# The first modulation's weights by tiles of 128 features, and three blocks of the first product row by row

## The chip, the cores and the metric

The kernel runs on one core of one Trainium2 chip. What is measured is the time of one execution on the device in microseconds (us). The kernel before takes 1365.48 us, the median of three runs (1364.51 to 1366.25).

## The reference

Three transformer layers for one sequence of 256 tokens with 1024 features, in float32. The first layer is an attention with a branch of pooled tokens beside it, then a gated feed-forward with a short convolution; the second has forgetting and sliding-window attention, the third a selected attention and eight experts. Every layer is modulated: a vector c gives, by a product with a weight of 1024 rows and 6144 columns, a shift, a scale and a gate for each of the two halves of the layer. What the change touches is the beginning:

```
mod = silu(c) @ ada_w + ada_b            # 6 x 1024: shift1, scale1, gate1, ...
h   = rms_norm(x, norm1_g) * (1 + scale1) + shift1
z   = h @ w_in                           # q, k, v, pooled part, two gates
q   = rms_norm(heads(q), q_norm_g);  k = rms_norm(heads(k), k_norm_g)
logits = q k^T * scale + bias_table[distance]
```

No column of z can be finished before all 1024 features of h are there, and a feature of h needs its own column of shift1 and of scale1.

## The kernel before

**Layout.** Features lie on partitions: x is four tiles of 128 x 2 x 256, eight "rows" of 128 features by 256 tokens. Every product with a weight is made in three float32r passes: weights and features are both split into a high part (ScalarE, `split_hi`, line 195) and a low part (VectorE, `split_lo`, line 198), and `mm3` (lines 214 to 216) multiplies high by high, high by low and low by high. One block of w_in (256 columns, 1 MB) is 48 matmuls of 256 columns: eight rows of features, two halves, three passes.

**The weights.** `Stream` holds one list of loads, `plan`. Each load is up to 1 MB into one of five buffers called `raw`, issued from the SP queue (line 89). A load is issued in the code whenever a buffer is handed out (`take`), and waits for the reader of the buffer that it overwrites. Weights of kind "w" are split ahead of their use into `whi` and `wlo`; the modulation's weights ("ada", "fill") are used whole.

**The modulation.** 8 MB hold shift1 and scale1: group 0 of layer 0, in eight pieces of 128 rows of ada_w by 2048 columns. `ada_step` (sum at line 344) multiplies each by silu(c), copied to 32 columns (`cb`), four matmuls of 512 columns on four strips of the array. The sums are complete when the eighth piece is through; `ada_turn` then turns them to columns by four transposes (line 368) and adds the bias (line 370).

**The order at the start.** `run` calls `setup` (column vectors, five loads of modulation weights, x, the first 128 columns of the constants), `rope_tables` (tables of sine and cosine for a later layer), five sums, `t5_table` (the bias table by distance, written to memory and read back), the sums of squares of x (line 473), a sixth sum. `layer1` then calls `norm_first`: the reciprocal root, the split of w_in block 0, two more sums, the turn, and eight features, each by three operations (lines 465, 466, 468). After that come the reads of the bias table (line 741), the other constants (line 785, with the matrices "blk" and "flip"), the bands of the pooling (line 760), and the blocks 0 (q), 2 (k) and 4 (v) of w_in one after the other. Behind a block, work that was put off is done by `flush`: for q and k the mean square by heads, a product with "blk" (line 798), followed by three ScalarE and three VectorE operations (lines 400 to 408, 800). Then `t5_end` turns the bias round by four products with "flip" (line 750), and `weave` runs the heads, whose scores (line 564) start, between further blocks.

**What sets the order.** The program is written with a layer that makes the semaphores and orders each engine's instructions by when they become ready and by their place in the code. Two engines are exempt: in all of this part ScalarE keeps the order of the code (`ORDER`: main "a"), and inside the block "start" TensorE keeps it (start "p").

Of the kernel before, what the change touches and what calls it, by code (L numbers as in the profile page):

```python
# [9 lines left out]
F32 = mybir.dt.float32  # L10
# [6 lines left out]
T = 256  # L17
# [5 lines left out]
_COLS = {}  # L23
# [47 lines left out]
class Stream:  # L71
    """Weights in the order of their loads: loaded ahead, split into two float32r parts ahead.
    The modulations' weights ("ada") take part whole; those of a kind "fill" wait until they are asked for."""
# [10 lines left out]
    def load(self, upto=None):  # L84
        """As many as there is room for"""
# [54 lines left out]

    def next(self, key, ahead=None, finish=True):
# [11 lines left out]
class Kernel:  # L153
# [84 lines left out]
    def gemm_t_steps(self, key, h, kt, n=256, fine=False):  # L238
        """[n columns of w on partitions (two tiles a bank), tokens]"""
# [17 lines left out]
    def gemm_t2(self, keys, h):  # L257
        """Blocks of 256 columns, a row of h at a time as it is made"""
# [10 lines left out]
    def flush(self):  # L269
        """Work put off so that the tensor engine needn't wait for it"""  # L270
# [7 lines left out]
    def gemm_n_steps(self, key, h, fine=False):  # L278
        """[tokens on partitions (two tiles), 256 columns of w]"""
# [15 lines left out]
    def gemm_narrow(self, hi, lo, h):  # L295
        """[8 columns of w on partitions, tokens]"""
# [18 lines left out]
    def ada_step(self, layer, g, kt, raw, defer, weigh):  # L315
        """128 rows of a group of modulations' weights. weigh: on the vector engine, summed over the rows later"""
# [41 lines left out]
    def ada_turn(self, a):  # L358
        """The sums, on every 32nd partition, go to a column for each 128 of them"""
# [14 lines left out]
    def ada_finish(self, upto=None):  # L374
        """One step of what is left to do for the oldest group, or all that a group needs"""
# [19 lines left out]
    def rstd(self, ps, shape, first=None):  # L395
        """-2 / root of a mean square; the gains make up for the -2. first: a factor that goes ahead, in place"""
# [22 lines left out]
    def norm_begin(self, gain, layer=None, scale_i=None):  # L419
        """The norm that follows the coming updates of x"""  # L420
# [16 lines left out]
    def norm_sum_first(self, k):  # L437
        n = self.nrm
        if k % 2 == 0:
            n["sq"][k // 2] = self.big()  # L440
        self.nc.scalar.activation(n["sq"][k // 2][:, k % 2], self.x[k // 2][:, k % 2], AF.Square)
        self.norm_sum(k)

    def norm_first(self):
        """The first norm: the modulation is the last to come"""
        nc, n = self.nc, self.nrm
        r = self.rstd(n["ms"][:, 0], (slice(None), 0))
        xr = []
        for i in range(4):
            xr.append(self.big())  # L450
            nc.vector.tensor_tensor(xr[i], self.x[i], r[:, None, :].to_broadcast([128, 2, T]), op=OP.mult)
        self.S.split(1)
        self.S.ada(2)
        self.ada_finish()
        gs = self.sp.tile([128, 8], F32, name="gs", bufs=2)
        nc.vector.scalar_tensor_tensor(gs, self.mods(0, 1), 1.0, self.gain("n1"), op0=OP.add, op1=OP.mult)
        shift = self.mods(0, 0)
        hh, hl = [], []
        for i in range(4):
            th, tl = self.big(F32R), self.big(F32R)  # L460
            hh.append(th)
            hl.append(tl)
            for j in range(2):
                k = 2 * i + j
                nc.scalar.activation(th[:, j], xr[i][:, j], AF.Identity, scale=gs[:, k:k + 1], bias=shift[:, k:k + 1])  # L465
                nc.vector.tensor_scalar(xr[i][:, j], xr[i][:, j], gs[:, k:k + 1], shift[:, k:k + 1], op0=OP.mult,
                                        op1=OP.add)
                nc.vector.tensor_tensor(tl[:, j], xr[i][:, j], th[:, j].bitcast(F32), op=OP.subtract)  # L468
        return hh, hl
# [65 lines left out]
    def acc_end(self, key, act, gate, n_ada):  # L535
        """The last rows: each feature tile goes on into the stream and its norm"""
# [33 lines left out]
    def attend(self, q, k, v, add, pair, sink=None, after=None):  # L570
        """One head, a stage at a time; a pair's second one ends both"""
# [62 lines left out]
    def pair_out(self):  # L634
        """Where two heads' results meet, and their split for the product that follows"""
# [18 lines left out]
    def setup(self):  # L654
# [4 lines left out]
        self.S.load()  # L659
# [1040 lines left out]
```

## Time and profile before

| | |
|---|---|
| median of the runs | 1365.48 us (1364.51 to 1366.25) |
| profiled execution, first to last instruction | 1360.7 us |
| TensorE busy | 1311.9 us, 96% |
| TensorE, loading of weights into the array | 1166.2 us, 86% |
| VectorE busy | 970.2 us, 71% |
| ScalarE busy | 737.6 us, 54% |
| read and written | 342.81 MB, mean 252 GB/s |

All times in the rows are of the profiled execution, from its first instruction on; the runs' median contains some 4.8 us beside that span. PE is TensorE, DVE is VectorE, ACT is ScalarE. SPq is the queue of SyncE, which issues the loads. In a timeline a row can stand for several instructions (x4), the second number is the time from the start of the first to the end of the last, and in brackets stands how long the engine was idle before it and what ended that. Matmuls are pipelined, so the distance between two starts, not the length of one, tells what one costs in a sequence. A float32 matmul stands there twice.

### The profile page before, as it was taken

The page shows a single profiled execution, that of the slowest core. Times are in us where ns is not written, and L with a number is a line of the kernel's source. Part 1 is how long each engine was busy: PE and PEld are TensorE (multiplying, and loading weights), DVE is VectorE, ACT ScalarE, POOL GpSimd, SP SyncE. Part 2 cuts the span into 40 slices and gives each one's busy share as a digit, 9 for nine tenths or more (in the row PEclk, how much of TensorE's full clock was granted, in tenths as well). Part 3 has the DMA queues.
Part 4 walks back from the last instruction along what each step waited for, and adds up shares of the span by engine and source line. Part 5 has one row for each costly group of instructions (what it writes and reads, how often), then busy time and mean ns, then how long its engine had stood idle before and what let it go on. Part 6 is the DMA issues. An engine that isn't in the chain of part 4 may idle for free. (4 is left out here: it accounts for less than half of the span.)

```text
span 1360.7 us, 22311 instructions
## 1 busy us (share of the span) xinstructions
PE 1311.9 (96%) x9230; PEld 1166.2 (86%) x9230; DVE 970.2 (71%) x1411; ACT 737.6 (54%) x928; POOL 4.1 (0%) x11
## 2 busy tenths in 40 slices
PE   5999999999999999999999999989999999999995
PEld 1777998899998887799999888669899899999994
DVE  3646865666567566666656579678889889889885
ACT  3645464544445454544334442656776776776773
POOL 0000000000000000000000000000000000000000
PEclk8899999999999999999999999999999999999997
DMA  9856947676664722577757553124998998997990
GB/s 370 333 194 245 407 188 274 232 284 233 266 226 188 302 97 76 192 300 301 279 216 278 193 225 109 48 93 177 351 355 293 350 374 283 341 371 276 348 374 34
DMA packets 54141, 342.81 MB, mean 252 GB/s; under 512 B 6061, under 2 KB 7349, under 8 KB 22928
## 3 DMA queue, kind: packets, MB, share of 16 engines
q1 hardware_dynamic: 53792, 341.02, 66.3%
q8 instruction: 74, 1.21, 0.4%
q0 software_dynamic: 240, 0.29, 0.2%
q14 instruction: 35, 0.29, 0.1%
HBM read 340.23 MB, written 1.06 MB: 251 GB/s over the span
## 5 line engine op out<-in xcount | busy, mean ns | idle before, releaser
L198 DVE TENSOR_TENSOR wlo<-raw,whi 128x2048 fp32r<-128x2048 f32 (+2 forms) x309 | 571.0, 1864 | 135.3 <-ACT whi L195 134.4
L195 ACT ACTIVATE whi<-raw 128x2048 fp32r<-128x2048 f32 (+2 forms) x309 | 482.7, 1573 | 181.8 <-PE ps L216 87.0
L214 PE MATMUL ps<-b,whi 128*128 128x256 f32 x1740 | 501.3, 289 | 1.2 <-ACT b L465 1.1
L215 PE MATMUL ps<-b,whi 128*128 128x256 f32 x1740 | 493.6, 284 | 0.5 <-DVE b L468 0.3
L216 PE MATMUL ps<-b,wlo 128*128 128x256 f32 x1740 | 493.1, 284 | 0.0
L214 PEld LDWEIGHTS ps<-b,whi 128*128 128x128 f32 x1740 | 333.7, 192 | 33.5 <-issue 16.1
L215 PEld LDWEIGHTS ps<-b,whi 128*128 128x128 f32 x1740 | 334.6, 192 | 3.2 <-issue 1.3
L216 PEld LDWEIGHTS ps<-b,wlo 128*128 128x128 f32 x1740 | 334.1, 192 | 1.8 <-issue 0.9
L215 PE MATMUL ps<-wlo,b 128*128 128x384 f32 (+2 forms) x800 | 267.0, 334 | 3.9 <-DVE wlo L198 3.9
L214 PE MATMUL ps<-whi,b 128*128 128x384 f32 (+2 forms) x800 | 267.0, 337 | 0.0
L216 PE MATMUL ps<-whi,b 128*128 128x384 f32 (+2 forms) x800 | 265.3, 332 | 0.0
L215 PEld LDWEIGHTS ps<-wlo,b 128*128 128x128 f32 x800 | 151.1, 189 | 13.7 <-DVE wlo L198 6.9
L214 PEld LDWEIGHTS ps<-whi,b 128*128 128x128 f32 x800 | 150.5, 189 | 9.0 <-issue 2.9
L216 PEld LDWEIGHTS ps<-whi,b 128*128 128x128 f32 x800 | 151.0, 189 | 7.3 <-issue 0.3
L344 PE MATMUL ps<-raw,cb 128*32 128x512 f32 x424 | 66.9, 639 | 14.3 <-DVE cb L672 9.4
L904 ACT ACTIVATE b<-ps,cols 128x256 f32<-128x256 f32 x44 | 24.7, 563 | 82.8 <-PE ps L216 53.5
L585 ACT ACTIVATE prob<-prob,tiny 128x128 f32<-128x128 f32 x80 | 35.7, 448 | 37.8 <-DVE tiny L580 20.7
L204 ACT ACTIVATE b<-b 128x512 fp32r<-128x512 f32 x24 | 15.2, 632 | 65.5 <-DVE b L929 44.6
L905 DVE SCALAR_TENSOR_TENSOR b<-ps,cols,b 128x255 f32<-128x255 f32 x44 | 21.2, 482 | 35.4 <-ACT b L904 35.3
L344 PEld LDWEIGHTS ps<-raw,cb 128*32 128x32 f32 x424 | 10.9, 111 | 38.9 <-DMA raw<-in_ada 13.5
L328 DVE SCALAR_TENSOR_TENSOR ada_acc<-raw,sc,ada_acc 128x2048 f32<-128x2048 f32 x16 | 37.5, 2347 | 4.6 <-DMA raw<-in_ada 4.5
L514 DVE SCALAR_TENSOR_TENSOR x<-ps,mod,x 128x256 f32<-128x256 f32 x72 | 31.1, 475 | 6.2 <-PE ps L216 5.8
(256 smaller groups left out, 977.8 us busy)
## 6 DMA issues: line engine op xcount, KB each, us to landing
raw<-in_ada SPq DMA_DIRECT2D x72, 1024.0 KB, 5.0
raw<-in_ed SPq DMA_DIRECT2D x40, 1024.0 KB, 7.7
raw<-in_eg SPq DMA_DIRECT2D x48, 768.0 KB, 5.6
raw<-in_eu SPq DMA_DIRECT2D x48, 768.0 KB, 5.5
raw<-in_w_up SPq DMA_DIRECT2D x22, 1024.0 KB, 5.5
raw<-in_w_in SPq DMA_DIRECT2D x16, 1024.0 KB, 7.0
raw<-in_w_down SPq DMA_DIRECT2D x11, 1024.0 KB, 6.8
raw<-in_e_fg SPq DMA_DIRECT2D x11, 1024.0 KB, 5.3
```

The costliest lines, as they stand in the source:

```text
L195: self.nc.scalar.activation(hi[:, c], raw[:, c], AF.Copy)
L198: self.nc.vector.tensor_tensor(lo[:, c], raw[:, c], hi[:, c].bitcast(F32), op=OP.subtract)
L204: nc.scalar.activation(hi, src, AF.Copy)
L214: mm(ps, ah, bh, start=start, stop=False, skip_group_check=True)
L215: mm(ps, ah, bl, start=False, stop=False, skip_group_check=True)
L216: mm(ps, al, bh, start=False, stop=stop, skip_group_check=True)
L328: nc.vector.scalar_tensor_tensor(a["acc"], raw, self.sc[:, c:c + 1], a["acc"], op0=OP.mult, op1=OP.add)
L344: self.nc.tensor.matmul(ps[32 * j:32 * j + 32, :], weights, rows[:, j * 512:(j + 1) * 512], start=start, stop=stop, skip_group_check=True)
L514: self.nc.vector.scalar_tensor_tensor(x, ps, gate[:, k:k + 1], x, op0=OP.mult, op1=OP.add)
L585: nc.scalar.activation(p[:, c], p[:, c], AF.Exp, bias=mn[:, t:t + 1], scale=-1.0, accum_out=sm[:, t:t + 1])
L904: nc.scalar.activation(y[:, j], ps[:, j], AF.Identity, scale=cw(2, j), bias=self.col("cb", base + j))
L905: nc.vector.scalar_tensor_tensor(y[:, j, 1:], ps[:, j, :T - 1], cw(1, j), y[:, j, 1:], op0=OP.mult, op1=OP.add)
```

## The change

The weights of shift1 and scale1 are laid out anew: `ada0f` holds eight tiles, tile k with all 1024 rows of the 128 shift columns and the 128 scale columns that feature row k needs. So one megabyte finishes one row of h. For each tile, `first_sums` makes eight matmuls of 256 columns, two on each of four strips of the array; `first_row` copies the four partial sums, adds and turns them by two matmuls with a column `pick` of zeros and four ones, adds the bias, makes the gain and finishes the features of the row with the three operations of before. `first_products` writes out the order: the sums of tile k, then the matmuls of blocks 0, 2 and 4 of w_in for row k - 1 (block 2 joins at tile 3, block 4 at tile 4 with the rows that it has missed), then the turn of tile k. The T5 table is made behind tile 4's turn. The plan loads tile 0, block 0, tile 1, block 2, tile 2, block 4, then tiles 3 to 7, then the rest as before. x is loaded ahead of the weights, and squared in tiles of 512. The constants are loaded in one piece where the second piece was loaded. The norm of q and of k, and the copy of v, follow the three blocks together; then one block of weights is split and the put-off work flushed. The rotary tables move to the second round of the first feed-forward. `first_row` uses the norm's result `xr` in place, as before.

```diff
@@ class Stream
+    def first(self):
+        raw = self.take(self.adas[self.n_a])
+        self.n_a += 1
+        return raw
@@ class Kernel
+    def first_sums(self, k):
+        nc = self.nc
+        raw, ps = self.S.first(), self.psum()
+        for kt in range(8):
+            j = 32 * (kt % 4)
+            nc.tensor.matmul(ps[j:j + 32, 0], self.cb[:, kt], raw[:, kt * 256:kt * 256 + 256], start=kt < 4,
+                             stop=kt >= 4, skip_group_check=True)
+        self.S.load()
+        return ps
+
+    def first_row(self, k, ps):
+        nc = self.nc
+        row = self.big()[:, 0]
+        nc.scalar.activation(row, ps[:, 0], AF.Copy)
+        for c in range(2):
+            nc.tensor.matmul(ps[:, 1, c:c + 1], row[:, c * 128:c * 128 + 128], self.pick, start=True, stop=True)
+        mod, gs = self.mod[0], self.gs0
+        o = _COLS["ab0"][0]
+        nc.vector.tensor_tensor(mod[:, k:16:8], ps[:, 1, 0:2], self.cols[:, o + k:o + 16:8], op=OP.add)
+        nc.vector.scalar_tensor_tensor(gs[:, k:k + 1], mod[:, 8 + k:9 + k], 1.0, self.gain("n1")[:, k:k + 1],
+                                       op0=OP.add, op1=OP.mult)
...
+        x, th, tl = (t[k // 2][:, k % 2] for t in (self.xr, *self.h0))
+        nc.scalar.activation(th, x, AF.Identity, scale=gs[:, k:k + 1], bias=mod[:, k:k + 1])
+        nc.vector.tensor_scalar(x, x, gs[:, k:k + 1], mod[:, k:k + 1], op0=OP.mult, op1=OP.add)
+        nc.vector.tensor_tensor(tl, x, th.bitcast(F32), op=OP.subtract)
+
+    def first_products(self):
+        S, h = self.S, self.h0
+        blocks = []
+
+        def weights(i, tokens):
+            blocks.append((self.parts(S.next(("w_in", i), 1, False), 8, 256), self.psum(), tokens))
+
+        def rows(b, ks):
+            (hi, lo), ps, tokens = blocks[b]
+            for k in ks:
+                for m in range(2):
+                    c = slice(m * 128, m * 128 + 128)
+                    if tokens:
+                        self.mm3(ps[:, m], h[0][k // 2][:, k % 2, c], h[1][k // 2][:, k % 2, c], hi[:, k], lo[:, k],
+                                 k == 0 and m == 0, k == 7)
+                    else:
+                        self.mm3(ps[:, m], hi[:, k, c], lo[:, k, c], *self.row(h, k), k == 0 and m == 0, k == 7)
+
+        self.first_row(0, self.first_sums(0))
+        weights(0, False)
+        for k, after in ((1, ((0, (0,)),)), (2, ((0, (1,)),)), (3, ((1, (0, 1)), (0, (2,)), (1, (2,)))),
+                         (4, ((2, (0, 1, 2)), (0, (3,)), (1, (3,)), (2, (3,)))),
+                         *((k, tuple((b, (k - 1,)) for b in range(3))) for k in (5, 6, 7)),
+                         (8, tuple((b, (7,)) for b in range(3)))):
+            if k < 8:
+                ps = self.first_sums(k)
+            for b, ks in after:
+                rows(b, ks)
+            if k < 8:
+                self.first_row(k, ps)
+            if k in (1, 2):
+                weights(2 * k, k == 2)
+            if k == 4:
+                self.t5_table()
+        self.flush()
+        return [ps for _, ps, _ in blocks]
@@ setup
-        self.S.load()
         self.x = [self.ap.tile([128, 2, T], F32, name=f"x{i}") for i in range(4)]
         for i in range(4):
             nc.sync.dma_start(self.x[i], d["xT"][:, 2 * i:2 * i + 2, :])
+        self.S.load()
         self.cst = self.cp.tile([128, N_CONST], F32, name="cst")
-        nc.sync.dma_start(self.cst[:, :128], d["cst"][:, :128])
@@ layer1
-    def layer1(self):
-        nc, x, S = self.nc, self.x, self.S
-        h = self.norm_first()
+    def layer1(self, first):
+        nc, S, h = self.nc, self.S, self.h0
         self.t5_begin()
-        nc.sync.dma_start(self.cst[:, 128:], self.d["cst"][:, 128:])
+        nc.sync.dma_start(self.cst, self.d["cst"])
         self.pool_bands()
...
-        qk_norm(0, *self.gemm_t2((("w_in", 0),), h))
-        self.whole(qk_piece(2))
-        self.whole(v_piece(0))
+        qk_norm(0, first[0])
+        qk_norm(2, first[1])
+        vn[0] = self.copy_out(first[2])
+        self.S.split(1)
+        self.flush()
         self.t5_end()
@@ ffn
+            if i == 1 and conv:
+                self.rope_tables()
@@ plan
-        plan += [("fill",) + x[1:] for x in ada[0][:6]] + l1[:1] + [("fill",) + x[1:] for x in ada[0][6:8]]
-        put(l1[1:], ada[0][8:24], 3)
+        first = [("first", k, d["ada0f"][k], 2048) for k in range(8)]
+        for k in range(3):
+            plan += [first[k], l1[k]]
+        plan += first[3:]
+        put(l1[3:], ada[0][8:24], 1)
@@ run
-                self.rope_tables()
...
-                S.ada(5)
-                self.t5_table()
-                for k in range(8):
-                    self.norm_sum_first(k)
-                S.ada(1)
+                for i in range(4):
+                    self.norm_squares(i)
+                    self.norm_sums(i)
+                self.norm_first()
+                first = self.first_products()
```

## Rows read from the trace of the kernel before

**Rows 1.** The page, part 1: TensorE's busy time, share, instructions; its weight loads; other engines.

```profile
PE 1311.9 (96%) x9230; PEld 1166.2 (86%) x9230; DVE 970.2 (71%) x1411; ACT 737.6 (54%) x928; POOL 4.1 (0%) x11
```

**Rows 2.** Timeline of TensorE, 15 to 64 us: start us, us, operation, idle before.

```profile
15.95 1.07 PE L344 MATMUL ps<-raw,cb 128*32 128x512 f32 x8 [0.85 <-DMA raw<-in_ada]
18.46 1.93 PE L344 MATMUL ps<-raw,cb 128*32 128x512 f32 x8 [1.45 <-DMA raw<-in_ada]
20.33 1.45 PE L729 MATMUL ps<-prob,rb 33*8 33x384 f32 x2
...
31.26 1.53 PE L344 MATMUL ps<-raw,cb 128*32 128x512 f32 x8 [1.42 <-DMA raw<-in_ada]
33.49 1.12 PE L368 MATMUL ps<-cst,b 128*128 128x128 f32 x4 [0.70 <-ACT b L356]
35.70 0.58 PE L214 MATMUL ps<-b,whi 128*128 128x256 f32 x1 [1.10 <-ACT b L465]
36.61 0.58 PE L215 MATMUL ps<-b,whi 128*128 128x256 f32 x1 [0.33 <-DVE b L468]
...
37.20 0.41 PE L214 MATMUL ps<-b,whi 128*128 128x256 f32 x1
37.42 0.41 PE L215 MATMUL ps<-b,whi 128*128 128x256 f32 x1
...
45.06 0.28 PE L214 MATMUL ps<-b,whi 128*128 128x256 f32 x1
45.18 0.28 PE L215 MATMUL ps<-b,whi 128*128 128x256 f32 x1
...
50.79 1.10 PE L798 MATMUL ps<-b,cst 128*128 128x512 f32 x2 [0.17 <-DMA cst<-in_cst]
...
57.47 1.02 PE L798 MATMUL ps<-b,cst 128*128 128x512 f32 x2
58.33 3.60 PE L750 MATMUL ps<-b,cst 128*128 128x512 f32 x8
...
63.34 0.46 PE L564 MATMUL ps<-b 64*128 64x128 f32 x2 [1.41 <-DVE b L800]
```

**Rows 3.** Busy time by stretch: TensorE, its loads, DVE, ACT, POOL, granted clock, DMA.

```profile
30.00:32.00 2.00, 0.74 (x8) 0.16 (x8) 2.00 (x5) 0.20 (x1) 0.00 (x0) 0.93 1.02 426
...
40.00:42.00 2.00, 2.00 (x11) 2.00 (x11) 1.97 (x5) 2.00 (x2) 0.96 (x2) 0.51 1.01 418
42.00:44.00 2.00, 2.00 (x19) 2.00 (x19) 2.00 (x2) 0.70 (x1) 0.12 (x1) 1.00 0.93 331
...
1346.00:1348.00 2.00, 0.00 (x0) 0.00 (x0) 0.69 (x1) 0.07 (x1) 0.00 (x0) 0.50 0.03 8
```

**Rows 4.** SP's queue: timeline of its loads, then its longest waits up to 70 us.

```profile
20.46 13.94 SPq L89 DMA_DIRECT2D raw<-in_w_in  x3
...
35.40 2.26 SPq L741 DMA_DIRECT2D b<-t5tab  x4
37.71 0.59 SPq L785 DMA_DIRECT2D cst<-in_cst  x1
39.02 8.22 SPq L760 DMA_DIRECT2D b<-in_band  x4
...
SPq L89 <- DVE wlo L198: 5.6, 1, 5.6
SPq L89 <- PE ps L344: 4.9, 2, 4.2
```

**Rows 5.** Timelines of DVE and ACT: a feature's low part, and two of a norm's steps.

```profile
35.69 0.41 DVE L466 TENSOR_SCALAR b<-b,gs,mod 128x256 f32<-128x256 f32 x1 [0.67 <-ACT b L465]
...
58.53 0.69 ACT L400 ACTIVATE b<-ps,eps 128x512 f32<-128x512 f32 x1 [2.21 <-PE ps L798]
...
59.91 0.63 ACT L402 ACTIVATE b<-b 128x512 f32<-128x512 f32 x1
```

**Rows 6.** The page, part 6: the modulation's loads, KB each, median us to landing.

```profile
raw<-in_ada SPq DMA_DIRECT2D x72, 1024.0 KB, 5.0
```

More of the change, by code (lines that the diff above doesn't have):

```diff
@@ L435, in norm_feed, with norm_squares @@
             nc.vector.tensor_scalar(n["xg"][i][:, j], self.x[i][:, j], n["gs"][:, k:k + 1], None, op0=OP.mult)
-    def norm_sum_first(self, k):
+    def norm_squares(self, i):
         n = self.nrm
[L439 to L442, printed above, removed]
+        n["sq"][i] = self.big()
+        self.nc.scalar.activation(n["sq"][i], self.x[i], AF.Square)
     def norm_first(self):
@@ L447, in norm_first @@
         r = self.rstd(n["ms"][:, 0], (slice(None), 0))
-        xr = []
+        self.xr = []
         for i in range(4):
[L450 to L468, printed above, removed]
@@ L469, in norm_first @@
-        return hh, hl
+            self.xr.append(self.big())
+            nc.vector.tensor_tensor(self.xr[i], self.x[i], r[:, None, :].to_broadcast([128, 2, T]), op=OP.mult)
+        self.mod[0] = self.cp.tile([128, 48], F32, name="mod0")
+        self.gs0 = self.sp.tile([128, 8], F32, name="gs", bufs=2)
+        self.h0 = ([], [])
+    def first_sums(self, k):
[7 more added lines that the diff above has]
+        return ps
@@ new lines, in first_row @@
+    def first_row(self, k, ps):
[9 more added lines that the diff above has]
+                                       op0=OP.add, op1=OP.mult)
+        if k % 2 == 0:
+            for part in self.h0:
+                part.append(self.big(F32R))
+        x, th, tl = (t[k // 2][:, k % 2] for t in (self.xr, *self.h0))
+        nc.scalar.activation(th, x, AF.Identity, scale=gs[:, k:k + 1], bias=mod[:, k:k + 1])
+        nc.vector.tensor_scalar(x, x, gs[:, k:k + 1], mod[:, k:k + 1], op0=OP.mult, op1=OP.add)
+        nc.vector.tensor_tensor(tl, x, th.bitcast(F32), op=OP.subtract)
@@ L674, in setup @@
         nc.vector.memset(self.ones, 1.0)
+        self.pick = self.cp.tile([128, 1], F32, name="pick")
+        nc.vector.memset(self.pick, 0.0)
+        for j in range(4):
+            nc.vector.memset(self.pick[32 * j:32 * j + 1], 1.0)
     def rope_tables(self):
@@ L1513, in run @@
                 self.norm_begin("n1")
-                S.ada(5)
-                self.t5_table()
-                for k in range(8):
-                    self.norm_sum_first(k)
-                S.ada(1)
+                for i in range(4):
[3 more added lines that the diff above has]
+                first = self.first_products()
             self.nsink = self.cp.tile([128, 8], F32, name="nsink")
             nc.vector.tensor_scalar(self.nsink, self.col("sink", 0, 8), -1.0, None, op0=OP.mult)
-            h = self.layer1()
+            h = self.layer1(first)
             self.ffn(h, ("w_up", "w_up2", "w_down"), self.mods(0, 5), True, lambda: self.norm_begin("en1", 1, 1))
@@ L1651, in _layout @@
         d[f"ada{l}"] = _ada(a[name][0])
+    w = a["ada_w"][0][:, :2048].reshape(8, 128, 2, 8, 128)
+    d["ada0f"] = np.ascontiguousarray(w.transpose(3, 1, 0, 2, 4)).reshape(8, 128, 2048)
     d["w_in"] = _by_cols(a["w_in"][0])
```

## The prediction

> **What bounds the kernel now.** I read the page's busy shares first: TensorE is busy for 1311.9 of 1360.7 us [rows 1], so all idle time together is 48.8 us, and no change that keeps the multiplications can win more. Then TensorE's timeline of the first 64 us, where the change lies. The reader is to see three stretches. Until 31.26 us TensorE waits for the modulation's megabytes, which land every 2.5 us (15.95, 18.46) [rows 2]; eight of them, x and one block of w_in are needed. From 35.70 it multiplies without a hole, one matmul each 0.21 us until about 41.9, then one each 0.12 us [rows 2]: the granted clock is at half (1.2 GHz) up to 42 us, after a stretch in which the engine was mostly waiting, and full (2.4 GHz) behind it [rows 3]. The three blocks end at 57.47, two products with the constant "blk" stand between and behind them, four with "flip" follow, and the first scores start at 63.34 [rows 2]. From there on TensorE has hardly a gap until the end. So **63.34 us is the number to beat**: what the change moves that point by, it moves the end by.
>
> Third, SP's timeline: loads leave in the order in which the program names them. For 13.9 us SP sits at three loads of w_in, mostly waiting for buffers that TensorE (4.9 us in all) and VectorE (5.6) have yet to read, and does not send the free loads of constants and bands meanwhile; those go out at 35.40, 37.71 and 39.02, in program order [rows 4]. The constants arrive just in time: "blk" waits 0.17 us for them at 50.79 [rows 2].
>
> **The change part by part.** Durations are those of the one profiled execution (span 1360.7 us); the runs' median lies 4.8 us above it, outside the work shown, and I add the difference to the median.
>
> *Arrival.* x takes the place that the first megabyte had. That one landed at 18.46 - 4 x 2.5 = 8.5 us; then come first0, w_in 0, first1, w_in 2, first2, w_in 4, first3 at 11.0, 13.5, ... 26.0. Two more megabytes (w_in 2 and 4) now lie before the last modulation tile, so DMA alone would bring that at about 36 us instead of 31.26 [rows 2].
>
> *TensorE from 26.0 on.* Before first3 little can be multiplied: 12 of the 144 matmuls. From there the written order makes TensorE the bound, and I sum it at full clock:
> - five sums of a tile, 5 x 1.07 = 5.4 (eight matmuls of 256 columns for four of 512: the same columns) [rows 2];
> - five turns of a row by two products with "pick". No row has them; above, the four transposes (1.12 at half clock, so 0.56) and below, nothing, as pick could lie in another's shadow [rows 2]. I take the transposes: 2.8;
> - the T5 table, now in here: 1.45 at half clock, 0.7 [rows 2];
> - 132 matmuls at 0.12: 15.8 [rows 2];
> - waits for the feature. From a finished turn it is mod, gain, high part on ScalarE, and the low part. Before, the turn ended at 34.6, the first matmul started at 35.70 and the second, which needs the low part, at 36.61 [rows 2]: 2.0 us. The low part's first step waits for ScalarE, 0.67 us [rows 5]. For tiles 4 to 6 a sum of 1.07 covers about half, 0.9 each is left; behind tile 7 nothing covers it. 3 x 0.9 + 1.9 = 4.6. If VectorE and ScalarE run ahead it is 0, at most 2.0 each, 10.
>
> Sum 29.3, so 55.3 us. Half clock: up to 26 us the engine works in shorter pieces than before, so I count one recovery as at 35.7 to 41.9, 6.2 us x (1 - 0.12/0.21) = 2.7 [rows 2, 3]; bounds 0 and the whole stretch. The three blocks end at **58.0 us**, not earlier than before: the hole is filled, but the sums' two halves, the chain of eight features and the extra turns eat it.
>
> *The constants.* This is what becomes late. "blk" and "flip" are now loaded whole behind the first product's code, so behind fifteen loads, the last of which (w_in 5) reuses the buffer of first7. Its sum ends two rounds of 18 matmuls, one turn and one feature's chain before the end: 58.0 - 2 x 2.2 - 0.5 - 1.9 = 51.2. From there a megabyte takes 5.0 us [rows 6] and lands at 56.2. Behind it come the T5 bias and the constants. Before, w_in 3 landed at 31.26 + 5 x 2.5 = 43.8 and the constants at 50.8, 7.0 us for both [rows 2, 4]; at the full 2.5 us a megabyte it would be 4.4. I take 7.0, the measured one: **63.2 us**. TensorE stands 5 us for "blk" (0 if the loads go out earlier, 7 at most).
>
> *What follows in place of the block that stood between.* Before, "blk" for q ran 6.7 us ahead of that for k, with a block between. Now both stand together: the first takes 1.1, then two chains of three ScalarE steps (58.53 to 60.54, 2.0 each), then VectorE's three for k up to the score at 63.34, 2.8 behind [rows 2, 5]: 1.1 + 4.0 + 2.8 = 7.9. The scores start at **71.1 us**, 7.8 later than before. TensorE's own 5.8 us (two "blk", four "flip") end 2.1 before that; matmuls of w_in 1, split by then, can fill it, since TensorE's order outside the start is found by readiness. That gives back between 0 and 2.1; I take 2.0. Net +5.8.
>
> *The stall's own price.* Near the end, where TensorE stands still from 1346 to 1348 us, its clock is at half [rows 3]. So behind a stall of 5 us "blk" and "flip" may run at half, up to 3 us more. I leave it out of the sum, since no row shows what a stall of just this length does, and keep it in the range.
>
> *Beside other work.* The rotary tables leave the start for the second round of the first feed-forward: nine VectorE and three ScalarE operations of 0.3 to 0.5 us, under a TensorE that has none of it in its own queue; cover gone, the price is their sum, some 4 us. x first, Squares of 512 for 256, the merged constants load, the memsets of pick: off the path, as x is there 2.5 us before the first tile. ScalarE has one block's split less done ahead at the scores; w_in 3's 4.2 us of splitting then lies under 48 matmuls. Zero, at most 2. The end of the program is untouched.
>
> **Where a rule speaks against it.** The clock rows show recovery after six unbroken microseconds [rows 3]; whether rounds of sums, waits and 18 matmuls count as unbroken no row shows. If TensorE stayed at half through them, 132 matmuls and five sums would take 16.7 us more than at full clock (132 x 0.09 + 5 x 0.9): the blocks end at 55.3 + 16.7 = 72, the last sum 10.4 before that at 61.6, the constants land at 73.6 and the scores start at 81.5, net +16 with the fill. The Trainium skill's "TensorE: Matmul & The Clock Gate", section "HAM oscillation — how this bites in real kernels", says that a loop whose computing per tile is shorter than its wait for the next tile falls back in clock on every tile. By that rule the trace agrees for the stretch before 31 us; after first3 the wait is the shorter one, so I give it little.
>
> **Rivals.** *Constants in time, net nothing*: SP sends them while it waits for buffers, or TensorE takes w_in 1 during the stall. Then the scores start 7.9 behind 58.0 at 65.9, less the fill of 2.0: +0.5 us, 1366. For it: nothing binds "blk" to the weights. Against it: SP's order before [rows 4]; and w_in 1 is split by ScalarE only behind the three blocks.
>
> *Faster*: the chain of features is hidden and the clock stays full from 26.0 on, with constants at 56 or before. 26.0 + 5.4 + 2.8 + 0.7 + 15.8 = 50.7, scores at 58.6, less 2.0: -6.7; with half of the feature waits and half of the recovery left, -3 to -4; I write 1361. It decides at whether SP's constants go out before the sum of tile 5, about 42 us. For it: ScalarE and VectorE are two thirds idle there. Against: in-place writing makes the low part wait for the high part [rows 5].
>
> *Clock at half throughout*: +16 us, 1382, as above. That the change doesn't overlap at all is no rival: the matmuls of tile 3 on can't be kept from running between loads.
>
> **How the numbers follow.** Forecast, slower by 3 to 10 us, 0.52; half clock throughout, 0.06; within 0.2% (2.7 us, about what can be told from no change), 0.21; faster, 0.21. The likeliest: 1365.5 + 5.8 = **1371.3 us**, its own range 1368.2 to 1375.5. The range for all, 1360.5 to 1377, leaves out the half-clock case and the better half of the faster one's tail.
>
> **What would show it.** Right: w_in 5's load leaves SP only after the sum of tile 7, near 51 us; the wait of "blk" for the constants is the largest of TensorE behind 26 us, about 5; the third block ends near 58; the first score starts near 71, and from there the two traces run alike. Wrong: constants landing before the third block ends, a score before 63 us, or a granted clock that stays full between 20 and 34 us; and a wait in the first feed-forward would show the rotary tables uncovered.

## The result: 12 us slower

The changed kernel takes 1377.27 us, the median of four runs (1375.75 to 1378.43), beside 1364.99 for the kernel before (four runs): a ratio of 1.0096, 95% interval 1.0080 to 1.0113. The forecast was 1371.3 with a range up to 1377, so the sign was right, the size about half of what came, and the result lies just past the end of the range. The profiled execution took 1376.16 us over a span of 1374.4, so 1.8 lie beside the span. The span of before was 1360.7; if 1.8 lay beside that too, it was a quick execution of some 1362.5, and not 4.8 us lay outside it as the text above says. Differences of spans below are therefore some 1.4 us larger than those of medians: 13.7 for 12.3.

TensorE's page line shows that 8.2 of the 13.7 us are busy time (1320.1 for 1311.9 in [rows 1]), so idle time is the smaller part of the loss. It has 92 more records: 64 of the tiles' sums, which come in halves, and 28 of the turns, which take 4.9 us together for the 1.12 of [rows 2]. Matmuls at half clock, shown further down, are busy for longer too:

```profile
PE 1320.1 (96%) x9322; PEld 1174.2 (85%) x9322; DVE 973.1 (71%) x1428; ACT 740.0 (54%) x929; POOL 4.0 (0%) x11
```

TensorE's timeline of the start, after, columns as in [rows 2] (L531 are the norm's sums, L466 a tile's sums, L477 a turn, L220 to L222 the three passes, L858 "blk", L811 "flip", L622 scores, L350 a later modulation's sums, L659 transposes in the heads):

```profile
8.61 5.04 PE L531 MATMUL ps<-b,ones_d 128*128 128x256 f32 x12 [0.96 <-ACT b L446]
13.58 1.07 PE L466 MATMUL ps<-raw,cb 128*32 128x256 f32 x16
...
21.26 0.58 PE L220 MATMUL ps<-b,whi 128*128 128x256 f32 x1 [3.45 <-ACT whi L201]
23.59 0.58 PE L222 MATMUL ps<-b,wlo 128*128 128x256 f32 x1 [1.53 <-DVE wlo L204]
...
29.61 1.93 PE L466 MATMUL ps<-raw,cb 128*32 128x256 f32 x16
...
46.00 0.50 PE L477 MATMUL ps<-pick,b 128*128 128x1 f32 x4
...
48.56 0.39 PE L221 MATMUL ps<-b,whi 128*128 128x256 f32 x1 [0.52 <-DVE b L489]
...
50.70 0.50 PE L477 MATMUL ps<-pick,b 128*128 128x1 f32 x4
51.13 1.07 PE L466 MATMUL ps<-raw,cb 128*32 128x256 f32 x16
52.63 0.38 PE L220 MATMUL ps<-b,whi 128*128 128x256 f32 x1 [0.42 <-ACT b L487]
...
57.32 0.38 PE L220 MATMUL ps<-b,whi 128*128 128x256 f32 x1 [1.15 <-ACT b L487]
...
60.23 0.28 PE L222 MATMUL ps<-whi,b 128*128 128x256 f32 x1
63.23 2.74 PE L858 MATMUL ps<-b,cst 128*128 128x512 f32 x4 [2.72 <-DMA cst<-in_cst]
65.77 4.55 PE L811 MATMUL ps<-b,cst 128*128 128x512 f32 x8
71.41 0.48 PE L622 MATMUL ps<-b 64*128 64x128 f32 x2 [1.09 <-DVE b L860]
...
82.05 1.05 PE L350 MATMUL ps<-raw,cb 128*32 128x512 f32 x2
83.03 0.44 PE L659 MATMUL ps<-cst,prob 128*128 128x128 f32 x2
83.40 1.06 PE L350 MATMUL ps<-raw,cb 128*32 128x512 f32 x6
```

The first scores start at 71.41, 8.1 us behind the 63.34 of [rows 2]. SP's queue, after, shows why "blk" stood still for 2.72 us: the constants leave behind w_in 5, and that behind the sum of the last tile (51.13 to 52.2); in [rows 4] they left at 37.71.

```profile
52.26 0.33 SPq L89 DMA_DIRECT2D raw<-in_w_in  x1
52.64 2.34 SPq L802 DMA_DIRECT2D b<-t5tab  x4
55.03 0.47 SPq L845 DMA_DIRECT2D cst<-in_cst  x1
```

Laying the same matmuls of both traces side by side gives the ledger: +8.1 us at the first scores, +9.2 from 84 us to 267, +13.8 from 280 on, and 13.6 at the end. So there are three steps, and two lie behind the first scores.

The step of 1.1: before, four sums on four strips of the array ran together (eight records, since a float32 matmul is two), as TensorE's timeline of the kernel before has it:

```profile
74.20 1.07 PE L344 MATMUL ps<-raw,cb 128*32 128x512 f32 x8
```

After, one stands at 82.05, then two transposes of the heads, and three at 83.40. Each group takes 1.05, so 2.1 in all. The six variants below that keep the changed kernel's order of loads (a1, a2, a6, c1, c2, c4) part one sum from three as well; d1 and d2, whose loads are ordered otherwise, and those of the kernel before don't.

The step of 4.6 us: ScalarE's timeline at the rotary tables, after, and TensorE's beside it:

```profile
274.44 0.42 ACT L760 ACTIVATE b<-b 128x256 f32<-128x256 f32 x1 [3.71 <-DVE b L753]
...
275.46 3.70 ACT L201 ACTIVATE whi<-raw 128x2048 fp32r<-128x2048 f32 x2
```

```profile
277.41 0.39 PE L220 MATMUL ps<-b,whi 128*128 128x256 f32 x1 [1.50 <-ACT whi L201]
...
279.21 0.52 PE L220 MATMUL ps<-b,whi 128*128 128x256 f32 x1 [1.30 <-ACT whi L201]
...
280.17 0.41 PE L220 MATMUL ps<-b,whi 128*128 128x256 f32 x1
280.38 0.41 PE L221 MATMUL ps<-b,whi 128*128 128x256 f32 x1
```

ScalarE keeps the code's order, so it stands 3.71 us before the tables' first step, which waits for the last of VectorE's nine; two splits of weights that TensorE needs stand behind it. TensorE waits 1.50 and 1.30, and then multiplies at 0.21 instead of 0.12 for some 3 us. The Trainium skill, page "PSUM — Partial Sum Buffer", section "Engine vs sequencer instructions", says that ScalarE's queue is strictly first in, first out; the trace agrees, as the two splits that stand behind the tables' first step sat out its 3.71 us.

The windows, columns as in [rows 3], show the clock at 1.2 GHz (0.50) from 20 to 30 us, where TensorE waits 3.45 and 1.53 us for the split of w_in 0, and partly so behind each of the two stalls:

```profile
20.00:30.00 10.00, 7.21 (x40) 5.41 (x44) 5.38 (x7) 4.14 (x5) 0.00 (x0) 0.50 0.88 339
30.00:40.00 10.00, 10.00 (x87) 8.32 (x79) 5.19 (x10) 3.63 (x5) 0.00 (x0) 0.82 1.00 381
...
42.00:50.00 8.00, 7.22 (x69) 5.21 (x68) 2.61 (x8) 1.94 (x4) 0.51 (x1) 1.00 0.63 220
50.00:60.00 10.00, 7.38 (x66) 6.23 (x65) 2.32 (x8) 2.17 (x5) 1.63 (x3) 1.00 0.83 274
60.00:70.00 10.00, 7.28 (x17) 3.08 (x15) 5.85 (x8) 8.15 (x12) 0.00 (x0) 0.83 0.95 357
...
280.00:295.00 15.00, 15.00 (x115) 14.03 (x115) 10.50 (x15) 8.12 (x9) 0.00 (x0) 0.91 0.59 216
```

### The profile page after: what moved, and what is told of

It is laid out like the page before. It is cut to its first block, busy times and chain, and to the rows that moved or that the text cites. A ratio compares the mean times of both kernels' runs of the same rounds, so it can differ in the third digit from the quotient of the medians.

```text
span 1374.4 us, 22525 instructions
## 1 busy us (share of the span) xinstructions
PE 1320.1 (96%) x9322; PEld 1174.2 (85%) x9322; DVE 973.1 (71%) x1428; ACT 740.0 (54%) x929; POOL 4.0 (0%) x11
## 5 line engine op out<-in xcount | busy, mean ns | idle before, releaser
L220 PE MATMUL ps<-b,whi 128*128 128x256 f32 x1740 | 502.5, 290 | 8.2 <-ACT whi L201 6.3
L222 PE MATMUL ps<-b,wlo 128*128 128x256 f32 x1740 | 493.6, 284 | 1.5 <-DVE wlo L204 1.5
L220 PEld LDWEIGHTS ps<-b,whi 128*128 128x128 f32 x1740 | 334.1, 192 | 43.6 <-issue 16.5
L222 PEld LDWEIGHTS ps<-b,wlo 128*128 128x128 f32 x1740 | 334.5, 192 | 3.7 <-DVE wlo L204 1.8
L220 PE MATMUL ps<-whi,b 128*128 128x384 f32 (+2 forms) x800 | 266.5, 336 | 0.0
L222 PE MATMUL ps<-whi,b 128*128 128x384 f32 (+2 forms) x800 | 265.1, 331 | 0.0
L221 PEld LDWEIGHTS ps<-wlo,b 128*128 128x128 f32 x800 | 151.1, 189 | 13.8 <-DVE wlo L204 7.3
L220 PEld LDWEIGHTS ps<-whi,b 128*128 128x128 f32 x800 | 150.5, 189 | 9.1 <-issue 3.1
L222 PEld LDWEIGHTS ps<-whi,b 128*128 128x128 f32 x800 | 151.0, 189 | 7.3 <-issue 0.3
L966 ACT ACTIVATE b<-ps,cols 128x256 f32<-128x256 f32 x44 | 24.7, 564 | 82.6 <-PE ps L222 52.2
L350 PE MATMUL ps<-raw,cb 128*32 128x512 f32 x360 | 55.9, 602 | 0.0
L531 PEld LDWEIGHTS ps<-b,ones_d 128*128 128x128 f32 x96 | 18.6, 211 | 20.5 <-ACT b L446 7.3
L531 PE MATMUL ps<-b,ones_d 128*128 128x256 f32 x96 | 28.7, 433 | 7.7 <-ACT b L446 6.5
```

Of the source, the lines that this page charges most:

```text
L220: mm(ps, ah, bh, start=start, stop=False, skip_group_check=True)
L221: mm(ps, ah, bl, start=False, stop=False, skip_group_check=True)
L222: mm(ps, al, bh, start=False, stop=stop, skip_group_check=True)
L350: self.nc.tensor.matmul(ps[32 * j:32 * j + 32, :], weights, rows[:, j * 512:(j + 1) * 512], start=start, stop=stop, skip_group_check=True)
L531: self.nc.tensor.matmul(n["ms"][:, 0], self.ones_d, n["sq"][k // 2][:, k % 2], start=k == 0, stop=k == 7)
L966: nc.scalar.activation(y[:, j], ps[:, j], AF.Identity, scale=cw(2, j), bias=self.col("cb", base + j))
```

## The experiments

Each ratio is against the kernel before, run on the same chip; the changed kernel's is 1.0096. "Shift" is how much later the same matmuls run than in the kernel before, both as profiled. "Norm's chain" is what follows "blk" up to the scores on ScalarE and VectorE. "Unread products" are small matmuls whose result nobody uses.

**The rotary tables.** Theory: ScalarE's wait for VectorE is the whole of the step of 4.6 us. a1 changes only that in the changed kernel: VectorE's part stays in the second round of the feed-forward, ScalarE's three operations go to the third. a3 is the kernel before with the tables moved as the change moves them, in one step; d3 is the same in two steps.

```diff
+        self.angles = ang, kk
+
+    def rope_sines(self):
+        nc = self.nc
+        ang, kk = self.angles
         nc.scalar.activation(kk, ang, AF.Abs)
...
             if i == 1 and conv:
                 self.rope_tables()
+            if i == 2 and conv:
+                self.rope_sines()
```

> The changed kernel, with the rotary tables in two steps: VectorE's chain in the second round of the first feed-forward, ScalarE's three operations in the third. Theory: ScalarE, which keeps the order of the code, stood idle for VectorE's chain there (3.7 us), the next weights were split late, and TensorE waited; with the chain done ahead that is gone: 3 to 3.5 us faster than the changed kernel, 8.5 to 9.5 us slower than before (ratio about 1.0065), and no wait of TensorE for the high parts near 278 us. Rival: the twelve operations themselves load engines that are already short there: unchanged, 12 us slower than before (1.009), the wait moves one round on.

> The kernel before with one part of the change alone: the rotary tables moved to the second round of the first feed-forward. Theory: this part alone costs what the traces differ by there, 3 to 3.6 us (ratio 1.0024), less what the freed start gives, at most 0.5. Rival: the difference came from the late start of everything ahead of it, and the move is free: within 1 us of before.

> The kernel before with the rotary tables alone moved, in two steps: VectorE's in the second round of the first feed-forward, ScalarE's in the third. Theory: the move in one step lost 4.8 us in the feed-forward and won about 1 at the start, since VectorE no longer waits there for the positions; in two steps the loss is gone: 0.5 to 2.5 us faster than before (ratio 0.998 to 0.9995). Rival: the work itself costs it there: 1.001 as in one step.

a1: 1373.18 us, ratio 1.0063 (1.0050 to 1.0076), 3.3 thousandths or 4.5 us below the changed kernel; its trace has no step at 270 us. The traces of a2, a6 and c1, which leave the tables as the change has them, have it, 4.5 to 4.8 us. The profiled execution of a1 was its slowest, 1380.44: TensorE waited 2.90 us for the norm before the scores and then ran partly at half clock until about 90 us, shift 16.1 before 270 us and after.

a3: 1365.87 us, ratio 1.0014 (1.0005 to 1.0022). Its ScalarE shows the same wait, though the start is another, and its shift goes from -0.9 (-2.4 at the scores, then a stretch at half clock) to +3.9:

```profile
264.41 0.42 ACT L699 ACTIVATE b<-b 128x256 f32<-128x256 f32 x1 [3.71 <-DVE b L692]
```

d3: 1361.37 us, ratio 0.9988 (0.9979 to 0.9997). The scores start at 60.98, 2.4 us earlier than before (the first sum, which waits for a copy that VectorE has behind the tables' first step, starts at 6.29 for 9.37), and nothing is lost in the feed-forward. So moving the tables is worth 2.4 us at the start, and costs 4.6 to 4.8 us in the traces if ScalarE's part follows directly on VectorE's; between the medians of a3 and d3 it is 2.6 thousandths, 3.5 us. d3 is the only kernel here that is quicker than the kernel before, by about 1.5 us.

**The constants and the third block.** Theory of a2: the late constants are the stall, so a load behind tile 3's turn gives it back. Theory of a6: with two blocks row by row and v behind them, v covers the wait for the constants. c2 joins both, flushes the norm's products ahead of v, and has the tables in two steps.

```diff
 # a2: the load moves up
+            if k == 3:
+                self.nc.sync.dma_start(self.cst, self.d["cst"])
...
         self.t5_begin()
-        nc.sync.dma_start(self.cst, self.d["cst"])
 # a6: two blocks, then v
-                         (4, ((2, (0, 1, 2)), (0, (3,)), (1, (3,)), (2, (3,)))),
-                         *((k, tuple((b, (k - 1,)) for b in range(3))) for k in (5, 6, 7)),
-                         (8, tuple((b, (7,)) for b in range(3)))):
+                         *((k, tuple((b, (k - 1,)) for b in range(2))) for k in (4, 5, 6, 7, 8))):
...
-        vn[0] = self.copy_out(first[2])
-        self.S.split(1)
-        self.flush()
+        self.whole(v_piece(0))
 # c2: both of these, the tables in two steps, and
+        self.flush()
+        self.whole(v_piece(0))
```

> The changed kernel, with the constants' load issued behind tile 3's turn, ahead of six later loads. Theory: the wait of 2.7 us for the constants and the half clock that follows it (two blk and part of four flip) are the price of loading them late: blk starts at once behind the third block, near 60.6, the first scores near 68.5 instead of 71.4, 2.5 to 3.5 us faster than the changed kernel (ratio to before about 1.0068). Rival: the T5 bias, still behind the last weights, is next, or the constants push the tiles back by their own 1.9 us: the first scores stay above 70.5, under 1 us faster.

> The changed kernel with two blocks (q, k) row by row instead of three; v's block is multiplied behind them as before. Theory: with three blocks all three pairs of split buffers are held to the end, so nothing is ready to cover the wait for the constants; with two, v's 5.8 us cover it and the next block's split is done beside them: the two blocks end near 55, blk starts near 61 without a wait, the first scores near 69, 2 to 3.5 us faster than the changed kernel (ratio to before about 1.007). Rival: fewer matmuls to a tile leave the feature's chain more exposed (0.9 us more a tile), which takes it back: the first scores stay at 71 or later, no gain.

> Two blocks row by row, constants loaded behind tile 3's turn, the two blk products ahead of v's block, so that its 5.8 us lie beside the norm's chain of 7.9 us, and the rotary tables in two steps. Theory: the price of the change is the sum of late constants, an uncovered chain and the wait for the rotary tables; all three gone, the scores start at about 55 + 2.2 + 5.8 + 3.6 = 66.6 without a wait of over 1 us, and nothing is lost in the feed-forward: 8 to 9 us faster than the changed kernel, 2 to 4 us slower than before (ratio 1.002 to 1.003). Rival: with a stall removed another takes its place (the T5 bias for flip, the split of v's block), and it stays above 1.006.

a2: 1375.36 us, ratio 1.0086 (1.0073 to 1.0100). "blk" no longer waits, but the scores do, for the norm's chain on VectorE, and they start at half clock (0.79 for 0.48):

```profile
57.62 1.88 PE L859 MATMUL ps<-b,cst 128*128 128x512 f32 x4
...
67.44 0.79 PE L624 MATMUL ps<-b 64*128 64x128 f32 x2 [4.52 <-DVE b L861]
```

Shift 4.1 at the scores, 7.2 soon after: the stall moved behind "blk" and grew. One reason stands in ScalarE's timeline, and it is that of the rotary tables again: the code has the split of w_in 1 ahead of the norm's first step, which therefore starts at 60.11, some 1.3 us after the first product with "blk" is there. In the changed kernel the same split lay under the wait for the constants (61.04 to 62.94).

```profile
58.31 1.90 ACT L201 ACTIVATE whi<-raw 128x2048 fp32r<-128x2048 f32 x1
60.11 0.68 ACT L406 ACTIVATE b<-ps,eps 128x512 f32<-128x512 f32 x1
```

The ratio is a thousandth, 1.4 us, below the changed kernel's, and the intervals overlap, so a gain isn't shown. The trace can't show it either: its first tile's sums start at 12.01 for 13.58 us, long before the moved load. Up to that point the changed kernel, a1, a2, a6 and c2 have the same code, and their traces spread there from 12.01 to 14.00 us.

a6: 1378.75 us (1374.62 to 1383.38), ratio 1.0102 (1.0081 to 1.0123), no gain. The scores come near the 69 us of the theory, but v, which ran ahead of "blk", covered only part of the wait for the constants and nothing of the norm's chain behind it. After the two waits TensorE ran at half clock (0.50 from 70 to 80 us): shift 6.1 at the scores, 13.3 soon after.

```profile
61.27 1.96 PE L858 MATMUL ps<-b,cst 128*128 128x512 f32 x4 [3.70 <-DMA cst<-in_cst]
...
69.44 0.66 PE L622 MATMUL ps<-b 64*128 64x128 f32 x2 [2.78 <-DVE b L860]
...
73.74 0.79 PE L622 MATMUL ps<-b 64*128 64x128 f32 x2
```

c2: 1368.29 us, ratio 1.0029 (1.0019 to 1.0039). TensorE has no wait between 54 and 80 us: "blk" runs as soon as k is through, v lies over the chain, and the scores come at 66.26.

```profile
55.16 1.99 PE L864 MATMUL ps<-b,cst 128*128 128x512 f32 x4
...
62.74 3.59 PE L818 MATMUL ps<-b,cst 128*128 128x512 f32 x8
66.26 0.48 PE L624 MATMUL ps<-b 64*128 64x128 f32 x2
```

The shift is 2.9 at the scores, 4.1 behind the parted strip sums, and stays there to the end. So the stall, the uncovered chain and the tables made some 9 of the 12 us; c2 takes the first two away together, and no run here parts them.

**The clock.** c1 is the changed kernel with small products that nothing reads, put into TensorE's waits; c3 is the kernel before with fourteen of them around the last two sums; it also has TensorE keep the code's order in `norm_first`. Theory: the half clock at the start costs several us that this gives back.

```diff
+    def warm(self, n):
+        ps = self.psum()
+        for _ in range(n):
+            self.nc.tensor.matmul(ps[:, 0, 0:128], self.ones_d, self.ones_d, start=True, stop=True)
```

> The changed kernel with float32 products of a constant, whose result nobody reads, put where TensorE waits: 9 ahead of the norm's sums, 14 behind tile 1's sums, 7 ahead of the last rows, 13 behind the third block, 5 behind flip. Theory: of the late start some 5 us are the clock at half (21 to 33 us, and again at blk and flip); kept busy, it stays full, the third block ends near 56 instead of 60.5 and the first scores start near 67: 3 to 5 us faster than the changed kernel (ratio to before about 1.0065). Rival: the waits for the split of w_in 0, the constants and the norm's chain alone set the start, the clock's share is hidden in them: under 1 us, or slower where a dummy delays a product.

> The kernel before with 14 such products where TensorE waits in the last 6 us ahead of the first block: 6 between the last two sums, 3 ahead of the turn, 5 behind it. Theory: there too the clock falls in those waits and half of the first block is multiplied at half clock, 6.2 us at half, 2.7 us lost; kept busy, the first block runs at full clock: 2 to 2.7 us faster than before (ratio 0.998). Rival: the clock falls all the same, or something else sets the end of the first blocks: no change.

c1: 1375.33 us, ratio 1.0084 (1.0069 to 1.0099). The window from 20 to 30 us has a granted clock of 1.00 instead of 0.50, and yet the scores start at 69.66, only 1.7 us earlier: the waits for the split, the features and the constants took the rest. The ratio's interval overlaps the changed kernel's.

c3: 1363.82 us, ratio 1.0003 (0.9993 to 1.0013), no difference. At full clock TensorE reaches "blk" too early for the constants:

```profile
50.09 1.10 PE L808 MATMUL ps<-b,cst 128*128 128x512 f32 x2 [1.48 <-DMA cst<-in_cst]
...
62.64 0.46 PE L573 MATMUL ps<-b 64*128 64x128 f32 x2 [1.41 <-DVE b L810]
```

**What is left of the start.** c4 is c2 with unread products and w_in 0 split ahead of the first turn. d1 multiplies only one block row by row, so that the constants can leave earlier and two splits can run ahead; d2 is d1 with unread products ahead of the norm, the early split, and a low part that is not written in place.

```diff
 # d1
-        for k in range(3):
-            plan += [first[k], l1[k]]
-        plan += first[3:]
-        put(l1[3:], ada[0][8:24], 1)
+        plan += [first[0], l1[0]] + first[1:]
+        put(l1[1:], ada[0][8:24], 3)
 # c4 and d2
-        self.first_row(0, self.first_sums(0))
+        ps = self.first_sums(0)
         weights(0, False)
+        self.first_row(0, ps)
```

> The two-block version with early constants and rotary tables in two steps, and besides w_in 0 split ahead of the first row's features (ScalarE kept the order row, split, and TensorE waited 5 us for it) and unread products in the waits at the start. Theory: the blocks start 2 to 3 us earlier and at full clock, the scores start at 61 to 63: within 2 us of before or faster by up to 2 (ratio 0.9985 to 1.0015). Rival: the loads of the eight tiles and two blocks set the pace then, as they did before: 1.003.

> The tiles of 128 features, but only block 0 of w_in row by row (its rows 0 and 1 behind the sums of tile 3, rows 2 and 3 behind tile 4, then one a tile), blocks 2 and 4 behind it as before, so that only one megabyte of w_in lies ahead of the last tile; the constants behind the load of w_in 1, the rotary tables in two steps. Theory: with three blocks a tile costs TensorE 1.07 + 0.5 + 2.2 us and the feature's wait, more than the 2.5 us in which it lands, so the start became bound by TensorE; with one block it costs 2.3 us and the load stays the bound: block 0 is done near 37 instead of 44.9, the first scores start at 56 to 59 instead of 63.3, 3 to 7 us faster than before (ratio 0.995 to 0.998). Rival: the chain of a feature (copy, turn, gain, split, some 2 us each, one after the other on three engines) and the clock at half hold the tiles back as they did with three blocks: block 0 is not done before 43 and the ratio is 1.000 or above.

> As the one-block version, and besides: unread products ahead of the norm's sums so that those run at full clock, w_in 0 split ahead of the first row's features, and the feature's low part made from a tile of its own instead of in place, so that it needn't wait for ScalarE (0.67 us each before). Theory: the chain of a feature is 0.5 us shorter and starts 2 to 3 us earlier: another 1 to 2 us faster than the one-block version where the chain binds, nothing where the load does. Rival: the split of w_in 0 ahead of the first feature delays it by its own 4.2 us: slower than the one-block version by 1 to 2 us.

c4: 1366.70 us, ratio 1.0024 (1.0012 to 1.0037), not told apart from c2. The scores start at 65.43, 0.8 earlier, and its profiled execution loses 2 us again between 840 and 1000 us.

d1: 1370.03 us, ratio 1.0044 (1.0028 to 1.0061). The rival was right that the tile's own chain holds the rounds back, though not alone. From turn to turn a round takes 3.26 us with 6 matmuls (37.77 to 41.03 below) and 4.70 with 18 (46.00 to 50.70 in the changed kernel). From the turn to the second matmul, which needs the feature's low part, it is 2.56 us in both (37.77 to 40.33, 46.00 to 48.56), and the rest of the matmuls adds to that, because the written order has the next turn behind them. So chain and matmuls follow each other instead of lying side by side; a turn placed ahead of the matmuls wasn't tried. Block 2 then waits for its split, which ScalarE's code has behind the square of block 0.

```profile
37.77 0.50 PE L477 MATMUL ps<-pick,b 128*128 128x1 f32 x4
...
40.33 0.39 PE L221 MATMUL ps<-b,whi 128*128 128x256 f32 x1 [0.52 <-DVE b L489]
...
41.03 0.50 PE L477 MATMUL ps<-pick,b 128*128 128x1 f32 x4
...
50.61 0.58 PE L220 MATMUL ps<-b,whi 128*128 128x256 f32 x1 [2.48 <-ACT whi L201]
```

d2: 1371.36 us, ratio 1.0055 (1.0042 to 1.0068), no gain over d1. The last six of the norm's eight sums (twelve records) take 2.86 instead of 5.04 us, the first tile's sums come at 11.55, and the chain from turn to low part is 2.12 us (36.57 to 38.69). The first scores start at 66.41, but the second ones at half clock, and the shift grows from 3.1 to 6.1. All five executions had a mean granted clock of 0.980 to 0.982 (d1 0.983 to 0.987).

```profile
8.28 2.86 PE L536 MATMUL ps<-b,ones_d 128*128 128x256 f32 x12 [1.11 <-ACT b L451]
11.55 1.07 PE L471 MATMUL ps<-raw,cb 128*32 128x256 f32 x16 [0.41 <-DMA raw<-in_ada0f]
...
69.41 0.79 PE L627 MATMUL ps<-b 64*128 64x128 f32 x2
```

**A better kernel before?** e1 joins d3, the unread products of c3 with its order of TensorE, and an early load of the constants.

```diff
-                S.ada(5)
+                S.ada(4)
+                self.nc.sync.dma_start(self.cst[:, 128:], self.d["cst"][:, 128:])
+                S.ada(1)
```

> The kernel before with the rotary tables moved in two steps, the unread products around the last two sums, and the second piece of the constants sent behind the fourth sum's code, ahead of w_in 2. Theory (in the kernel before the clock's recovery is worth 6.2 x 0.43 = 2.7 us, and only the constants, which came 1.5 us late, took it away): 'blk' finds its constants, the first scores start at 60.98 - 2.7 = 58.3 us, and the ratio falls from 0.9988 to 0.997. Rival (the split of the weights by ScalarE and VectorE ends last as soon as TensorE is faster, as the two waits of 0.5 us for low parts said): the scores start no earlier than 60 us, and the ratio stays at 0.998 to 0.999.

e1: 1365.18 us (1360.27 to 1369.10), ratio 1.0012 (1.0001 to 1.0023): rather a thousandth lost, where theory and rival both had a gain. The profiled execution was its quickest, with the scores at 59.84, close to the rival's 60:

```profile
47.36 1.02 PE L812 MATMUL ps<-b,cst 128*128 128x512 f32 x2
...
59.84 0.46 PE L573 MATMUL ps<-b 64*128 64x128 f32 x2 [1.41 <-DVE b L814]
```

Its mean granted clock was 0.993, and 0.983 in the slowest of the twelve. Where the others lost their clock no trace shows, so why e1 isn't quicker than d3 stays open.

## Where the prediction was right and where it failed

The sum up to the first scores came out, 71.1 for 71.41, partly by luck. What failed lies beside and behind it: the fill of 2.0 us didn't come, the rotary tables, put at nothing, cost 4.6, and parted strip sums, which the sum didn't have, cost 1.1.

- *first3 at 26.0, the blocks' end at 58.0.* They came at 29.61 and 60.51. The place was wrong, the stretch between right (30.9 us for 32.0). What failed is "Before first3 little can be multiplied": the norm's sums, at half clock, pushed the first tile's from 11.0 to 13.58, and the split of w_in 0 added waits of 3.45 and 1.53. d2 took away the half clock of the sums (first tile at 11.55); c4, with the split ahead of the first turn, has a wait of 2.53 for that turn in place of the two. The feature waits came near the 4.6 us of the sum: the low part's wait of 0.52 and the high part's of 0.42 and 1.15 are in the rows. The clock was back at 33.5 us, about as forecast, and not at half throughout. The Trainium skill, "TensorE: Matmul & The Clock Gate", section "HAM oscillation — how this bites in real kernels", tells of a loop whose computing per tile is shorter than its wait for the next tile, and whose clock falls on every tile. Behind 33.5 us the waits were the shorter part here (7.22 us busy of 8, 7.38 of 10), and the clock of 1.00 from 42 to 60 us agrees.
- *The constants land at 63.2.* "blk" started at 63.23. The mechanism (w_in 5 behind tile 7's sum, then the T5 bias and the constants) stands. That it fits so closely is luck: the load of w_in 5 left at 52.26 for 51.2, and 11.0 us followed for 12.0. The stall was 2.72 for 5 only because the blocks ended later.
- *Scores at 71.1.* 71.41: from "blk" to the scores it was 8.2 us for 7.9. "blk" and "flip" ran partly at half clock, but a1, where they didn't, took 8.3, so the norm's chain sets it.
- *The fill of 2.0 us.* **Wrong**: 0. No matmul of w_in 1 ran between "flip" and the scores. The three blocks hold all three pairs of split buffers to their end, so the split of w_in 1 begins on ScalarE at 61.04, and on VectorE here, ending at 65.3:

```profile
62.98 2.29 DVE L204 TENSOR_TENSOR wlo<-raw,whi 128x2048 fp32r<-128x2048 f32 x1 [4.80 <-ACT whi L201]
```

It was done 6 us ahead of the scores, and yet its matmuls stand behind the first of them (72.25) in TensorE's order. What failed is "can fill it, since TensorE's order outside the start is found by readiness". In c2, where the code names v's block ahead of "flip", matmuls do fill that place. Why those of w_in 1 stood behind stays open: a buffer of PSUM, of which the kernel has eight (line 183 of the changed one), could have held them back too, as one of the products with "flip" waited 0.2 us for ScalarE's copy of an earlier one.
- *The rotary tables at nothing.* **Wrong**, and the largest miss: 4.6 us (a1: about 4.5). That TensorE "has none of it in its own queue" is true and isn't the question; ScalarE has it in its queue, ahead of the splits. The price that the prediction named for lost cover, some 4 us, is near, but by another sum: not the operations' own time, but two waits for splits, 2.8 us, and the half clock behind them.
- *"From there the two traces run alike."* Wrong by the parted strip sums, 1.1 us, and by the tables.

Together: 8.1 + 1.1 + 4.6 = 13.8 by spans, where the forecast had 7.8 - 2.0 = 5.8. Of the rivals, constants in time (a2) brought 1.4 us by the medians, not told apart from nothing, and not 5: the norm's chain was waiting behind them. What c2 leaves, 2.9 us at the scores, I put down to the tile rounds, eight chains through three engines where one chain served all features before; no run shows that alone. They may cost more than the 2.9: c2 also has the tables out of the start, which is worth 2.4 us in the kernel before (d3), so by estimate 5.3 at the scores, and its ratio lies 4.1 thousandths, 5.6 us, above d3's.

## What to carry to other kernels

Work moved out of a busy start isn't free where it lands: look for the engine that keeps the code's order, and at what stands behind the moved instruction in its queue; if the step crosses engines, put what the second engine does one round later (4.5 us here). When a load is sent in program order, its time is that of the last buffer wait ahead of it, so an early constant belongs ahead of the loads that wait; but removing one stall pays only down to the next chain, so sum the second wait too. Where a loop alternates a chain through several engines with the products that need it, check whether the written order lets them overlap at all (2.56 us of chain and the matmuls, one after the other, here). Don't count a hole as filled because an order could fill it; have the code name the work ahead of it, as c2 does.

## What the runs showed that I had not expected

A stall of TensorE can cost more than its length, and not the same each time: behind waits of 2.8 to 4.5 us the scores ran at half clock (a1, a2, a6). Behind waits of 1.41 or 1.42 the second scores did so in a3, d1 and d2, and not in the kernel before, c3, d3 and e1. a3 and d3 have the same code up to the feed-forward, and both wait 1.42 us ahead of scores at 60.94 and 60.98; yet the granted clock from 61 to 64 us is 0.69 in a3's trace and 1.00 in d3's. a3's shift grows by 1.5 us there. So a shift read from a single trace can hold 1 to 2 us of chance.

Three of these kernels spread by 9 us (a1 1371.62 to 1380.44, a6 1374.62 to 1383.38, e1 1360.27 to 1369.10), and their quickest and slowest executions differ in the mean granted clock (0.986 and 0.979, 0.985 and 0.978, 0.993 and 0.983). Four strip sums take 1.07 us together and 2.1 when the order parts one from three. And a full clock early on is worth little where other waits bind: c1 has 1.00 for 0.50 from 20 to 30 us, and its scores start 1.7 us earlier.
